# A hybrid encoder layer on one core: the first projection by input chunk, four output tiles side by side

## The chip, the cores and the metric

The kernel runs on one core of one Trainium2 chip. The metric is the time of one execution on the device in microseconds (us); lower is better. The numbers shown with a run are the median, the lowest and the highest of its executions. One more execution was recorded by the hardware profiler, instruction by instruction; its rows are what this document reads.

The engines are named as in the profile: PE (TensorE, matmuls), PEld (its weight loads), DVE (VectorE), ACT (ScalarE), POOL (GpSimd), SP (SyncE, which here only starts transfers). A queue with a small q behind the engine's name is the part of the engine that issues.

## What is computed

A layer takes x of 512 tokens by 1024 features (float32). One RMS-normalised input feeds three token mixers: an attention with forget gates ("fox"), a gated delta net ("gdn") and a stick-breaking attention. Their outputs are gated, summed and projected; then come a cross attention into 256 memory tokens and a gated MLP with a causal convolution. The change touches the input of the first mixer stage. From the reference, cut to that:

```python
h = rmsnorm(x, norm_mix[l])      # x * rsqrt(mean(x^2) + eps) * gain
(fq, fk, fv, ff, gq, gk, gv, gb, ga, gz, sq, sk, sv, gates) = split_projection(h @ w_in[l])
qkv = jax.nn.silu(causal_dwconv(jnp.concatenate([gq, gk, gv], axis=-1), gdn_conv[l]))
cq, ck, cv = jnp.split(qkv, [GDN_KW, 2 * GDN_KW], axis=-1)
o = gated_delta_rule(l2norm(heads(cq, GDN_HEADS)), l2norm(heads(ck, GDN_HEADS)),
                     heads(cv, GDN_HEADS), g_log, beta)
```

gq, gk and gv are 512 features each, that is four output tiles of 128 features by 512 tokens.

## The kernel before, in words

**Data and precision.** Features lie on partitions, tokens along the free axis. x arrives in eight chunks x0 to x7 of 128 x 512 (256 KB each). All dense weights arrive as a stream of units of 128 x 1024 float32 (512 KB) in the order of use. A unit of the gdn projections holds one output tile: its eight blocks of 128 x 128 belong to the eight input chunks, so one output tile needs one unit and all of x.

**Products.** A float32 value is kept as an exact sum of two fp32r values, high and low. For a unit, `split_unit` (L148) makes the high part with a copy on ACT (L154, whi) and the low part with a subtraction on DVE (L155, wlo). For an x chunk, `split_scaled` does it with the norm's gain multiplied in (xh on ACT L167, xl on DVE L168). `mm3` (L171) adds three products per chunk: high by high (L175), high weights by low x (L176), low weights by high x (L178). So `project` (L183) issues 24 matmuls of 128 x 512 for an output tile.

**Buffers.** PSUM has three pools: three "dense" buffers for projections, three "misc" ones and two of the gdn stage. The weight stream has three raw buffers, two of high parts and two of low parts.

**The start.** SP issues every transfer: x0, then the packed parameters cols (L281), the first gk unit in two halves (L142, L143), and so on with x and the next units between each other, and last the constants const (L285). ACT's first instruction is the load of a function table (L111). For each x chunk the kernel makes xh, xl and the square (L296), and DVE sums the squares (L298). A matmul with ones gives their sum over features (xps, L301); a logarithm, an exponential, a square on ACT and a Newton step on DVE make r_x, the norm's factor for each token (L303).

**Projections.** `project_conv` does gk, gq and gv by `ORDER`, a string of steps: K (gk), k (its convolution), Q, q, N (normalise), V, v, R (per-head scalars) and so on. gk and gq are "deferred": they use x times gain, and r_x is multiplied in when PSUM is evicted (L337, DVE). gv and all later projections use the normalised input, which `normalize` makes in one go for the eight chunks: scale by gain and r_x on DVE (L322), high part on ACT (L323), low part on DVE (L324). gv is evicted by a plain copy on ACT (L339). The convolution of a tile is one product on ACT (L347) and three multiply-adds on DVE (L349); its silu runs in place on ACT, four tiles behind one table load (`in_one_go`, L117).

**Who sets the order.** A tile scheduler orders the instructions of each engine by dependence, priority and a simulated timeline. Where the program says so (`keep_in_program_order`, `issue_after`), it keeps the written order. So a change in one place can move instructions at others.

Of the kernel before, what the change touches and what calls it, by code (L numbers as in the profile page):

```python
# [21 lines left out]
DEFERRED = ("gk", "gq")  # L22
CROSS = "k0 q0 k1 q1 w0 k2 q2 w1 k3 q3 w2 w3 v"
ORDER = """K k Q q N V v R F0 p0 p1 f0 S0 p2 p3 F1 s0 e f1 F2 f2 A0 C0 l0 F3 l1 l2 S1 l3 S2 f3 s1 n0
# [7 lines left out]
H = 4  # L32
# [34 lines left out]
def build(nc, tc, ctx, x_t, mem_t, w, cols_d, const_d, unit_d, out_t, dbg=None):  # L67
# [14 lines left out]
    work = tiles_of("work", "n", 4)        # short-lived  # L82
# [22 lines left out]

    def dump(name, ap):
        if dbg is not None and name in dbg:
            nc.sync.dma_start(dbg[name], ap)
# [28 lines left out]
    units = {}  # L137

    def load_unit(u):
        raw = wp.tile([P, 1024], F32, tag="wraw", name=f"wraw{u}", bufs=WB[0])  # L140
        if u == 0:
            nc.sync.dma_start(raw[:, :T], w[u, :, :T])  # L142
            nc.sync.dma_start(raw[:, T:], w[u, :, T:])  # L143
        else:
            nc.sync.dma_start(raw, w[u])
        return raw

    def split_unit(u):  # L148
        """a unit of the weight stream as an exact sum of two float32r operands"""
        raw = units.pop(u) if u in units else load_unit(u)  # L150
        hi = wp.tile([P, 1024], F32R, tag="whi", name=f"whi{u}", bufs=WB[1])
        lo = wp.tile([P, 1024], F32R, tag="wlo", name=f"wlo{u}", bufs=WB[2])
        for s in [slice(0, T), slice(T, 2 * T)] if u == 0 else [slice(0, 2 * T)]:
            S.activation(hi[:, s], raw[:, s], AF.Copy)  # L154
            V.tensor_tensor(lo[:, s], raw[:, s], hi[:, s].bitcast(F32), ALU.subtract)  # L155
        return hi, lo

    def split(src, alloc, name):
        """src as hi + lo"""
# [11 lines left out]
    def mm3(ps, unit, blocks, xs, first, last):  # L171
        """ps += the blocks of a unit times xs, without the product of the low parts"""
# [30 lines left out]
    def project_heads(u, ys, name, n=4):  # L203
        """[512, 1024] weights, two output tiles in a unit"""
# [7 lines left out]
    def rsqrt(ps, name, scale, n=T, work=work):  # L212
        """-2 / sqrt(ps * scale + eps), with a Newton step"""
# [9 lines left out]
    def head_norm(src, name, scale, n=T, work=work, psum=misc_ps, light=False):  # L223
        """-2 / sqrt(sum of src^2 * scale + eps) on every partition"""
# [62 lines left out]
    V.tensor_scalar(gains, gains, -0.5, None, ALU.mult)  # L287
    G.memset(ones, 1.0)
    V.tensor_copy(ones_r, ones)

# [1 line left out]
    xs, acc = [], None  # L292
    for k in range(KC):
        sq = work(f"xsq{k}")
        xs.append(split_scaled(hs[k], gkeep(f"xh{k}", F32R), gkeep(f"xl{k}", F32R), col("norm_mix", k)))
        S.activation(sq, hs[k], AF.Square)  # L296
        if acc is not None:
            V.tensor_tensor(sq, sq, acc, ALU.add)  # L298
        acc = sq
    ps = misc_ps("xps")  # L300
    PE.matmul(ps, ones, acc, start=True, stop=True)  # L301
    r_x = cp.tile([P, T], F32, tag="rh", name="r_x")
    V.tensor_scalar(r_x, rsqrt(ps, "rx", 1.0 / D), -0.5, None, ALU.mult)  # L303
# [4 lines left out]
    V.tensor_copy(ident_b, ident)  # L308
    mkt = cp.tile([P, P], BF16, tag="mkt", name="mkt")
    V.tensor_copy(mkt, cst("mask_t"))  # L310
    mkt2 = mkt[:, None, :].to_broadcast([P, 4, P])

    def v4(t):
        return t.rearrange("p (a b) -> p a b", a=4)

    def normalize():
        for k in range(KC):
            if k % 4 == 0:
                two = hquad(f"hh{k // 4}", F32R), hquad(f"hl{k // 4}", F32R)
            hi, lo = two[0][:, k % 4], two[1][:, k % 4]  # L320
            t = hs[k]
            V.scalar_tensor_tensor(t, t, col("norm_mix", k), r_x, ALU.mult, ALU.mult)  # L322
            S.activation(hi, t, AF.Copy)  # L323
            V.tensor_tensor(lo, t, hi.bitcast(F32), ALU.subtract)  # L324
            hs[k] = hi, lo
# [5 lines left out]
    def project_conv(g):  # L331
        raws[g] = []
        for h in range(H):
            u = UNITS[g] + h
            t = ytile(f"{g}u{h}")
            if g in DEFERRED:
                V.tensor_tensor(t, project(u, xs, f"{g}{h}"), r_x, ALU.mult)  # L337
            else:
                S.activation(t, project(u, hs, f"{g}{h}"), AF.Copy)  # L339
            raws[g].append(t)  # L340

    def convolve(g, base):
        """silu(conv(projection)) of the tiles of q, k or v"""
# [17 lines left out]
    def scalars():  # L361
# [16 lines left out]
        S.activation(ncoef[:R], col("row_alog", 0, 0, R), AF.Exp)  # L378
# [8 lines left out]
        # token on partition: [.., token block, row]  # L387
# [5 lines left out]
        # beta, beta * exp(gc), exp(g_last - gc)  # L393
# [4 lines left out]
    def select(ps, kind, h, stop=True):  # L398
        """a row of the scalars on every partition"""
# [5 lines left out]
        if kind == "-c":  # L405
            V.tensor_scalar(sel[:R], unit(h), -1.0, None, ALU.mult)
        else:
            V.tensor_copy(sel[:R], unit(64 + h))
# [11 lines left out]
    def prep_head(h):  # L420
# [6 lines left out]
        # the decay, [j, i] by chunks, 0 for j > i  # L427
# [13 lines left out]
        # A^T without its factors beta_i, and attn^T  # L441
# [15 lines left out]
        # token-major keys and values  # L457
# [13 lines left out]
    # the inverses of the 32 x 32 diagonal blocks of I + A by elimination, a block's  # L471
    # even or odd columns on a partition
# [30 lines left out]
    def expand(dst, src, h):  # L503
        """the 32 x 32 blocks of a head on the diagonals of its chunks"""
# [63 lines left out]
    def qkv_head(u, h, name, norm, alloc):  # L568
        """q^T, k^T and [key, dv] by key blocks"""
# [20 lines left out]
    def packed(name, kinds):  # L590
        """[P, 128], .. [P, 512] of each kind, the halves of a kind's tile shared"""
# [78 lines left out]
    tri_r = cp.tile([P, 2, P], F32R, tag="tri_r", name="tri_r")  # L670
    V.tensor_copy(tri_r[:, 0], cst("tri"))
# [61 lines left out]
    for step in ORDER.split():  # L733
# [5 lines left out]
         "N": lambda h: normalize(), "R": lambda h: scalars(), "z": lambda h: silu_gate(),  # L739
# [187 lines left out]
def unit_columns():  # L927
    """[P, 32, 16]: the even (on even partitions) or odd columns of the unit matrix"""
# [4 lines left out]
def layout(inputs):  # L933
# [3 lines left out]
    def tiles(a, n):  # L937
        """[K, M] -> [units, P, 1024] streaming (output tile, k chunk) blocks of [P, 128]"""
# [88 lines left out]
```

## Time and profile before

| | us |
|---|---|
| median of three runs | 1073.2 |
| lowest, highest | 1072.76, 1074.09 |
| span of the profiled execution | 1072.4 |
| PE busy | 1055.4 (98%) |
| DVE busy | 638.3 (60%) |
| ACT busy | 556.3 (52%) |

The profiled execution is not timed apart from its profile; its span from the first to the last instruction is 1072.4 us, 0.8 us under the median of the runs. A share of busy time is an average over the whole span. A row of a timeline gives the start and the duration of one instruction or of a few like ones in a row, then engine, line, operation, the tile written and the tiles read, and in brackets how long the engine stood before it and for whom. Matmuls are pipelined and their ends are modelled, so the distance between two starts says more than a duration.

### The profile page before, as it was taken

What the parts mean: (1) busy time and instruction counts of PE and PEld (TensorE: products, weight loads), DVE (VectorE), ACT (ScalarE), POOL (GpSimd) and SP (SyncE); (2) the same over time, 40 slices, a digit from 0 to 9 for tenths busy, and PEclk for the clock granted to TensorE, in tenths of its full rate; (3) what the DMA queues carried; (4) which work ended last, traced back from release to release, by engine and by line L of the source; (5) the groups of instructions that cost most, each with busy time, mean ns of one, the idle gap of its engine ahead of it and who ended that gap; (6) DMA issues with size and microseconds to landing.
All of it is one profiled execution on the core that took longest, in us unless ns stands there. A gap on an engine that the chain in (4) does not pass through costs nothing.

```text
span 1072.4 us, 12705 instructions
## 1 busy us (share of the span) xinstructions
PE 1055.4 (98%) x4868; PEld 858.3 (80%) x4868; DVE 638.3 (60%) x1002; ACT 556.3 (52%) x894; POOL 31.6 (3%) x81
## 2 busy tenths in 40 slices
PE   6999999999999999999999998999999999999998
PEld 4887888778888888888888886778888888888886
DVE  5987566886454443454577667667776667742221
ACT  6689677856263646574546557544444444431110
POOL 0000100101010000000000000000000000000000
PEclk9999999999999999999999999999999999999999
DMA  5232212121211122122244233122222222233330
GB/s 209 79 98 98 79 61 77 61 88 59 80 59 60 59 64 74 60 65 97 94 147 168 90 107 99 41 97 99 90 90 95 98 99 92 91 103 108 118 117 20
DMA packets 27853, 96.33 MB, mean 90 GB/s; under 512 B 3088, under 2 KB 3344, under 8 KB 27536
## 3 DMA queue, kind: packets, MB, share of 16 engines
q1 hardware_dynamic: 27648, 95.26, 27.1%
q8 instruction: 38, 0.62, 0.2%
q10 hardware_dynamic: 144, 0.26, 0.1%
q14 instruction: 23, 0.19, 0.1%
HBM read 93.41 MB, written 2.10 MB: 89 GB/s over the span
## 4 chain that ended last, share of the span: by engine, by line
PE 96%; DVE 1%; ACT 1%; DMA 1%; issue 0%; SPq 0%; DVEq 0%; ACTq 0%
PE up L176 8%; PE up L178 8%; PE up L175 8%; PE g L176 4%; PE g L175 4%; PE g L178 4%; PE dn L178 4%; PE dn L176 4%; PE dn L175 4%; PE wo L176 1%; PE s L175 1%; PE f L178 1%; PE f L175 1%; PE s L176 1%; PE wo L178 1%; PE wo L175 1%
## 5 line engine op out<-in xcount | busy, mean ns | idle before, releaser
L154 ACT ACTIVATE whi<-wraw 128x1024 fp32r<-128x1024 f32 (+1 forms) x168 | 177.1, 1054 | 286.0 <-PE up L176 86.1
L155 DVE TENSOR_TENSOR wlo<-wraw,whi 128x1024 fp32r<-128x1024 f32 (+1 forms) x168 | 204.7, 1219 | 144.2 <-PE dn L178 49.2
L176 PE MATMUL up<-xfl,whi 128*128 128x512 f32 x352 | 139.3, 396 | 0.0
L175 PE MATMUL up<-xfh,whi 128*128 128x512 f32 x352 | 138.7, 394 | 0.0
L178 PE MATMUL up<-xfh,wlo 128*128 128x512 f32 x352 | 88.9, 395 | 0.0
L178 PEld LDWEIGHTS up<-xfh,wlo 128*128 128x128 f32 x352 | 66.3, 188 | 15.7 <-issue 0.2
L176 PEld LDWEIGHTS up<-xfl,whi 128*128 128x128 f32 x352 | 66.3, 188 | 15.7 <-issue 0.2
L175 PEld LDWEIGHTS up<-xfh,whi 128*128 128x128 f32 x352 | 66.3, 188 | 15.5
L175 PE MATMUL g<-hh,whi 128*128 128x512 f32 x192 | 76.9, 401 | 0.0
L176 PE MATMUL g<-hl,whi 128*128 128x512 f32 x192 | 76.8, 400 | 0.0
L889 DVE SCALAR_TENSOR_TENSOR uc<-u,cols,uc 128x511 f32<-128x511 f32 (+1 forms) x88 | 65.3, 747 | 1.4
L887 ACT ACTIVATE uc<-u,cols 128x512 f32<-128x512 f32 x44 | 35.8, 816 | 45.2 <-DVE u L885 45.0
L885 DVE TENSOR_TENSOR u<-up,r_f 128x512 f32<-128x512 f32 x44 | 30.2, 688 | 40.4 <-PE up L178 40.4
L178 PE MATMUL g<-hh,wlo 128*128 128x512 f32 x192 | 52.3, 402 | 0.0
L178 PEld LDWEIGHTS g<-hh,wlo 128*128 128x128 f32 x192 | 35.9, 188 | 8.3 <-issue 0.2
L176 PEld LDWEIGHTS g<-hl,whi 128*128 128x128 f32 x192 | 36.2, 188 | 7.8 <-issue 0.2
L175 PEld LDWEIGHTS g<-hh,whi 128*128 128x128 f32 x192 | 36.2, 188 | 7.7
L175 PE MATMUL f<-hh,whi 128*128 128x512 f32 x64 | 26.0, 406 | 0.0
L175 PE MATMUL s<-hh,whi 128*128 128x512 f32 x64 | 25.7, 402 | 0.0
L176 PE MATMUL s<-hl,whi 128*128 128x512 f32 x64 | 25.5, 398 | 0.0
L176 PE MATMUL wo<-msl,whi 128*128 128x512 f32 x64 | 25.3, 396 | 0.0
L176 PE MATMUL f<-hl,whi 128*128 128x512 f32 x64 | 25.3, 395 | 0.0
(968 smaller groups left out, 2288.1 us busy)
## 6 DMA issues: line engine op xcount, KB each, us to landing
wraw<-w SPq DMA_DIRECT2D x166, 512.0 KB, 3.3
x<-x_t SPq DMA_DIRECT2D x8, 256.0 KB, 7.2
xr<-x_t SPq DMA_DIRECT2D x2, 1024.0 KB, 6.2
out<-out SPq DMA_DIRECT2D x8, 256.0 KB, 2.0
mem_sb<-mem_t SPq DMA_DIRECT2D x4, 256.0 KB, 6.5
wraw<-w SPq DMA_DIRECT2D x2, 256.0 KB, 4.7
inv<-unit ACTq DMA_DIRECT2D x1, 256.0 KB, 3.9
const<-const SPq DMA_DIRECT2D x1, 194.0 KB, 6.4
```

What stands on the lines that cost most here:

```text
L154: S.activation(hi[:, s], raw[:, s], AF.Copy)
L155: V.tensor_tensor(lo[:, s], raw[:, s], hi[:, s].bitcast(F32), ALU.subtract)
L175: PE.matmul(ps, hi[:, b], xh, start=first and i == 0, stop=False)
L176: PE.matmul(ps, hi[:, b], xl, start=False, stop=False)
L178: PE.matmul(ps, lo[:, b], xh, start=False, stop=last and i == len(xs) - 1)
L885: V.tensor_tensor(u, ps, r_f, ALU.mult)
L887: S.activation(c, u, AF.Identity, bias=col("ffn_conv_b", j), scale=col("ffn_conv", 3 * j + 2))
L889: V.scalar_tensor_tensor(c[:, s:], u[:, :T - s], col("ffn_conv", 3 * j + 2 - s), c[:, s:], ALU.mult, ALU.add)
```

## The change

- A small transfer `gains0` (128 x 8, the norm's gains) goes first on SP. Then come the eight x chunks, and only then cols and const.
- The gk weights are laid out by input chunk (`tokens`): a unit now holds two input chunks, each with 512 output features. Each unit comes in two halves of 128 x 512. The halves of the first three units are issued by ACT, those of the fourth by SP.
- Nine matmuls of constants (`WARM`, ones_r by ones_r into the buffer of xps) stand ahead of the first gk product.
- The four gk tiles are accumulated side by side in two dense and two gdn buffers. For each chunk: high part of the weights and xh on ACT, low part and xl on DVE, then twelve matmuls; the squares follow one chunk behind. All of this is pinned in the written order. xps follows behind the last gk product.
- Small DVE operations on constants, which the scheduler had put between the sums of squares, are pinned behind r_x.
- gq and gv both use x times gain, and both are evicted by DVE with r_x multiplied in.
- `normalize` works on one chunk. A table puts the chunks behind the evictions of gq1, gq2, gq3, gv0 and gv1; the step N is gone from `ORDER`.

The diff, without comments and with what the prediction speaks of:

```diff
-DEFERRED = ("gk", "gq")
+WARM = 9
+NORMALIZE = {"gq1": (0, 1), "gq2": (2,), "gq3": (3, 4), "gv0": (5,), "gv1": (6, 7)}
-ORDER = """K k Q q N V v R F0 ...
+ORDER = """K k Q q V v R F0 ...
...
+    gains0 = cp.tile([P, KC], F32, tag="gains0", name="gains0")
+    nc.sync.dma_start(gains0, cols_d[:, COLS["norm_mix"]:COLS["norm_mix"] + KC])
     hs = []
     for k in range(KC):
         t = ptile(f"x{k}")
         nc.sync.dma_start(t, x_t[:, k])
         hs.append(t)
-        if k == 0:
-            nc.sync.dma_start(cols, cols_d)
-        if k in (0, 2, 5):
-            u = UNITS["gk"] + len(units)
-            units[u] = load_unit(u)
-    nc.sync.dma_start(const, const_d)
+    def load_chunks(g, queue):
+        raw = wp.tile([P, 1024], F32, tag="wraw", name=f"wraw{g}", bufs=WB[0])
+        for q in range(2):
+            queue.dma_start(raw[:, q * T:q * T + T], w[UNITS["gk"] + g, :, q * T:q * T + T])
+        return raw
+    chunk_raws = [load_chunks(g, nc.scalar) for g in range(3)]
     exp_ln_tables()
...
+    nc.sync.dma_start(cols, cols_d)
+    nc.sync.dma_start(const, const_d)
+    ps_x = misc_ps("xps")
+    for _ in range(WARM):
+        PE.matmul(v4(ps_x), ones_r, ones_r[:, None, :].to_broadcast([P, 4, P]), start=True, stop=True)
+    first = [dense_ps("gk0"), dense_ps("gk1"), gdn_ps("gk2"), gdn_ps("gk3")]
...
+        pin(S.activation(hi[:, s], raw[:, s], AF.Copy))
+        pin(S.activation(xh, hs[k], AF.Copy, scale=gain))
+        pin(V.tensor_tensor(lo[:, s], raw[:, s], hi[:, s].bitcast(F32), ALU.subtract))
+        pin(V.scalar_tensor_tensor(xl, hs[k], gain, xh.bitcast(F32), ALU.mult, ALU.subtract))
+        if k:
+            add_squares(k - 1)
+        for a, b in ((hi, xh), (lo, xh), (hi, xl)):
+            for h in range(H):
+                c = q * T + h * P
+                pin(PE.matmul(first[h], a[:, c:c + P], b, start=k == 0 and a is hi and b is xh, stop=k == KC - 1 and b is xl))
+    add_squares(KC - 1)
+    pin(PE.matmul(ps_x, ones, sums[-1], start=True, stop=True))
...
-            if g in DEFERRED:
-                V.tensor_tensor(t, project(u, xs, f"{g}{h}"), r_x, ALU.mult)
+            if g == "gk":
+                V.tensor_tensor(t, first[h], r_x, ALU.mult)
             else:
-                S.activation(t, project(u, hs, f"{g}{h}"), AF.Copy)
+                evict = V.tensor_tensor(t, project(u, xs, f"{g}{h}"), r_x, ALU.mult)
+                with tc.issue_after(evict.ins):
+                    for k in NORMALIZE.get(f"{g}{h}", ()):
+                        normalize(k)
...
-    put("gk", tiles(wi[:, 2052:2564], 4))
+    put("gk", tokens(wi[:, 2052:2564]))
```

How the change moves instructions shows at three places.

The first is the start of ACT's queue, before and then changed. In brackets are the semaphores that an instruction waits for; DMAHW ones are counted up by transfers that have landed, eight of them in turn (DMAHW1 by gains0, DMAHW3 by the second half of the first unit). wraw is a raw unit, ghi its high part.

```order
L111 ACT_TABLE_LOAD
L296 ACTIVATE xsq_121<-x_92 128x512 [waits DMAHW0_49]
L167 ACTIVATE xh_122<-x_92,cols 128x512 [waits DMAHW1_49]
L378 ACTIVATE ncoef<-cols 96x1
L154 ACTIVATE whi_204<-wraw_95 128x512 [waits DMAHW2_49]
L154 ACTIVATE whi_204<-wraw_95 128x512 [waits DMAHW3_49]
```

```order
L283 DMA wraw_110<-w 128x512 x2
L283 DMA wraw_113<-w 128x512 x2
L283 DMA wraw_116<-w 128x512 [waits DMAHW1_49]
L283 DMA wraw_116<-w 128x512 [waits DMAHW3_49]
L115 ACT_TABLE_LOAD
L318 ACTIVATE ghi_138<-wraw_110 128x512 [waits DMAHW0_49]
L319 ACTIVATE xh_140<-x_94,gains_92 128x512 [waits DMAHW2_49]
```

The table load, first before, now stands behind six issues, of which the last two wait.

The second place is DVE around r_x, before and then changed. gku is the evicted gk tile, identb, mkt, tri_r and sel_g are small constants.

```order
L219 SCALAR_TENSOR_TENSOR rxb<-xps,rxb 128x512
L220 SCALAR_TENSOR_TENSOR rxa<-rxb,rxa 128x512
L303 TENSOR_SCALAR r_x<-rxa 128x512
L337 TENSOR_TENSOR gku_202<-gk_203,r_x 128x512
L337 TENSOR_TENSOR gku_235<-gk_236,r_x 128x512
```

```order
L217 SCALAR_TENSOR_TENSOR rxa<-rxb,rxa 128x512
L331 TENSOR_SCALAR r_x<-rxa 128x512
L332 TENSOR_SCALAR cols<-cols 128x5
L337 CAST identb<-const 128x128
L339 CAST mkt<-const 128x128
L702 CAST tri_r<-const 128x128
L439 CAST sel_g_954<-const 96x128
L439 CAST sel_g_1042<-const 96x128
L364 TENSOR_TENSOR gku_342<-gk_134,r_x 128x512
```

Six small operations have come between r_x and the first eviction.

The third place is ACT where the norms of the gdn heads (gkn0, gqn0) meet the silus of gk, gq and gv, before and then changed.

```order
L117 ACTIVATE gk_333<-gk_333 128x512
L111 ACT_TABLE_LOAD
L347 ACTIVATE gq_489<-gqu_421,cols 128x512
L154 ACTIVATE whi_610<-wraw_608 128x1024
L216 ACTIVATE gkn0a<-gkn0p,cols 128x512
L217 ACTIVATE gkn0a<-gkn0a 128x512
L218 ACTIVATE gkn0b<-gkn0a 128x512
L347 ACTIVATE gq_490<-gqu_454,cols 128x512
L117 ACT_TABLE_LOAD
```

```order
L350 ACTIVATE hh_521<-x_104 128x512
L213 ACT_TABLE_LOAD
L213 ACTIVATE gkn0a<-gkn0p,cols 128x512
L151 ACTIVATE whi_720<-wraw_718 128x1024
L214 ACT_TABLE_LOAD
L214 ACTIVATE gkn0a<-gkn0a 128x512
L215 ACTIVATE gkn0b<-gkn0a 128x512
L223 ACTIVATE gqn0s<-gq_526 128x512
L121 ACT_TABLE_LOAD
L121 ACTIVATE gq_528<-gq_528 128x512
```

The logarithm and the exponential of gkn0 now each have a load of their own. Up to the last silu of the gv tiles ACT's queue held 9 table loads before and holds 13 now.

## Rows read from the trace of the kernel before

**Rows 1.** The page: busy time of each engine; then the chain that ended last.

```profile
PE 1055.4 (98%) x4868; PEld 858.3 (80%) x4868; DVE 638.3 (60%) x1002; ACT 556.3 (52%) x894; POOL 31.6 (3%) x81
...
PE 96%; DVE 1%; ACT 1%; DMA 1%; issue 0%; SPq 0%; DVEq 0%; ACTq 0%
```

**Rows 2.** Waits of PE: us in total, times, longest us.

```profile
PE gk L175 <- ACT whi L154: 6.4, 2, 6.2
...
PE mT L840 <- DVE mp L836: 2.5, 1, 2.5
```

**Rows 3.** Waits of PE between 30 and 640 us.

```profile
PE pk L446 <- DVE gqn3b L219: 0.3, 1, 0.3
```

**Rows 4.** Timeline of SP's issues at the start: start us, duration us, what.

```profile
0.81 0.39 SPq L278 DMA_DIRECT2D x<-x_t  x1
```

**Rows 5.** Timeline of ACT at the start.

```profile
3.89 0.63 ACT L296 ACTIVATE xsq<-x 128x512 f32<-128x512 f32 x1 [1.80 <-DMA x<-x_t]
...
7.90 0.63 ACT L154 ACTIVATE whi<-wraw 128x512 fp32r<-128x512 f32 x1 [1.78 <-DMA wraw<-w]
9.19 0.72 ACT L167 ACTIVATE xh<-x,cols 128x512 fp32r<-128x512 f32 x1 [0.66 <-DMA x<-x_t]
```

**Rows 6.** Timeline of PE, start to the first matmul of gq.

```profile
9.96 0.79 PE L175 MATMUL gk<-xh,whi 128*128 128x512 f32 x1 [2.57 <-ACT xh L167]
...
13.23 0.63 PE L176 MATMUL gk<-xl,whi 128*128 128x512 f32 x1
13.66 0.63 PE L175 MATMUL gk<-xh,whi 128*128 128x512 f32 x1
...
24.64 1.02 PE L301 MATMUL xps<-xsq,ones 128*128 128x512 f32 x2
...
34.82 2.03 PE L178 MATMUL gk<-xh,wlo 128*128 128x512 f32 x8
36.69 0.40 PE L175 MATMUL gq<-xh,whi 128*128 128x512 f32 x1
```

**Rows 7.** Windows: busy us (instructions) of each engine, granted clock, DMA engines' share, GB/s.

```profile
0.00:4.00 4.00, 0.00 (x0) 0.00 (x0) 0.36 (x2) 1.39 (x2) 0.42 (x5) 1.00 0.48 140
4.00:8.00 4.00, 1.22 (x2) 0.50 (x2) 1.61 (x3) 1.96 (x5) 0.00 (x0) 1.00 0.76 209
```

**Rows 8.** Timeline of DVE at the start.

```profile
1.05 0.23 DVE L289 CAST ones_r<-ones 128x128 fp32r<-128x128 f32 x1 [1.05 <-POOL ones L288]
```

**Rows 9.** Timeline of PE in the cross attention, on both sides of its wait for mp.

```profile
662.73 1.89 PE L829 MATMUL msc<-memk,mqT 128*128 128x256 f32 x8
...
668.01 3.50 PE L829 MATMUL msc<-memk,mqT 128*128 128x256 f32 x8 [0.30 <-DVE mm L834]
```

**Rows 10.** Windows, the stretch of the second of these groups; columns as in rows 7.

```profile
668.00:671.00 3.00, 2.99 (x7) 2.47 (x8) 1.45 (x4) 0.34 (x1) 0.00 (x0) 0.50 0.00 0
```

**Rows 11.** Groups of DVE's instructions, 12 to 24 us: busy us, mean ns, idle before.

```profile
L168 DVE SCALAR_TENSOR_TENSOR xl<-x,cols,xh 128x512 fp32r<-128x512 f32 x6 | 4.5, 744 | 0.0
...
L671 DVE CAST tri_r<-const 128x128 fp32r<-128x128 f32 x1 | 0.2, 218 | 0.0
```

**Rows 12.** Timeline around r_x: ACT's first step and DVE's first evictions behind it.

```profile
25.69 0.69 ACT L216 ACTIVATE rxa<-xps,cols 128x512 f32<-128x512 f32 x1 [1.61 <-PE xps L301]
...
29.66 1.29 DVE L337 TENSOR_TENSOR gku<-gk,r_x 128x512 f32<-128x512 f32 x2
```

**Rows 13.** Groups of ACT's instructions, 60 to 100 us, columns as in rows 11.

```profile
L154 ACT ACTIVATE whi<-wraw 128x1024 fp32r<-128x1024 f32 x7 | 7.4, 1052 | 1.4 <-PE gv L176 1.4
L117 ACT ACT_TABLE_LOAD x3 | 3.8, 1283 | 0.1
...
L339 ACT ACTIVATE gvu<-gv 128x512 f32<-128x512 f32 x4 | 2.4, 596 | 2.3 <-PE gv L178 2.3
```

**Rows 14.** Windows of 10 us from 60 to 120: the fourth, and the sum of the six.

```profile
90.00:100.00 10.00, 10.00 (x47) 8.15 (x46) 4.93 (x7) 9.81 (x13) 0.00 (x0) 1.00 0.15 52
...
sum 60.00, PE 60.00 PEld 47.98 DVE 42.61 ACT 50.26 POOL 2.89; mean PE 10.00 PEld 8.00 DVE 7.10 ACT 8.38 POOL 0.48
```

More of the change, by code (lines that the diff above doesn't have):

```diff
@@ L104, in gdn_ps, with v4 @@
         return pg.tile([P, T], F32, tag="g", name=name)
+    def v4(t):
+        return t.rearrange("p (a b) -> p a b", a=4)
     def dump(name, ap):
@@ L134, in build @@
     ones_r = cp.tile([P, P], F32R, tag="ones_r", name="ones_r")
-    units = {}
     def load_unit(u):
         raw = wp.tile([P, 1024], F32, tag="wraw", name=f"wraw{u}", bufs=WB[0])
[L141 to L145, printed above, removed]
+        nc.sync.dma_start(raw, w[u])
         return raw
     def split_unit(u):
-        raw = units.pop(u) if u in units else load_unit(u)
+        raw = load_unit(u)
         hi = wp.tile([P, 1024], F32R, tag="whi", name=f"whi{u}", bufs=WB[1])
         lo = wp.tile([P, 1024], F32R, tag="wlo", name=f"wlo{u}", bufs=WB[2])
-        for s in [slice(0, T), slice(T, 2 * T)] if u == 0 else [slice(0, 2 * T)]:
-            S.activation(hi[:, s], raw[:, s], AF.Copy)
-            V.tensor_tensor(lo[:, s], raw[:, s], hi[:, s].bitcast(F32), ALU.subtract)
+        S.activation(hi, raw, AF.Copy)
+        V.tensor_tensor(lo, raw, hi.bitcast(F32), ALU.subtract)
         return hi, lo
@@ L286, in build @@
     exp_ln_tables()
-    V.tensor_scalar(gains, gains, -0.5, None, ALU.mult)
     G.memset(ones, 1.0)
     V.tensor_copy(ones_r, ones)
-    xs, acc = [], None
-    for k in range(KC):
[L294 to L301, printed above, removed]
+    nc.sync.dma_start(cols, cols_d)
@@ new lines, in build, with add_squares @@
+    nc.sync.dma_start(const, const_d)
[3 more added lines that the diff above has]
+    first = [dense_ps("gk0"), dense_ps("gk1"), gdn_ps("gk2"), gdn_ps("gk3")]
+    pin = tc.keep_in_program_order
+    xs, sums = [], []
+    def add_squares(k):
+        sq = work(f"xsq{k}")
+        pin(S.activation(sq, hs[k], AF.Square))
+        if sums:
+            pin(V.tensor_tensor(sq, sq, sums[-1], ALU.add))
+        sums.append(sq)
@@ new lines, in build @@
+    for k in range(KC):
+        g, q = divmod(k, 2)
+        if q == 0:
+            raw = chunk_raws[g] if g < 3 else load_chunks(g, nc.sync)
+            hi = wp.tile([P, 1024], F32R, tag="whi", name=f"ghi{g}", bufs=WB[1])
+            lo = wp.tile([P, 1024], F32R, tag="wlo", name=f"glo{g}", bufs=WB[2])
+        s = slice(q * T, q * T + T)
+        xh, xl = gkeep(f"xh{k}", F32R), gkeep(f"xl{k}", F32R)
+        xs.append((xh, xl))
+        gain = gains0[:, k:k + 1]
+        pin(S.activation(hi[:, s], raw[:, s], AF.Copy))
[8 more added lines that the diff above has]
+                pin(PE.matmul(first[h], a[:, c:c + P], b, start=k == 0 and a is hi and b is xh, stop=k == KC - 1 and b is xl))
@@ L302, in build @@
+    add_squares(KC - 1)
+    pin(PE.matmul(ps_x, ones, sums[-1], start=True, stop=True))
     r_x = cp.tile([P, T], F32, tag="rh", name="r_x")
-    V.tensor_scalar(r_x, rsqrt(ps, "rx", 1.0 / D), -0.5, None, ALU.mult)
+    V.tensor_scalar(r_x, rsqrt(ps_x, "rx", 1.0 / D), -0.5, None, ALU.mult)
+    pin(V.tensor_scalar(gains, gains, -0.5, None, ALU.mult))
     gl = cp.tile([P, H, 4], F32, tag="gl", name="gl")
@@ L307, in build, with normalize @@
     ident_b = cp.tile([P, P], BF16, tag="identb", name="identb")
-    V.tensor_copy(ident_b, ident)
+    pin(V.tensor_copy(ident_b, ident))
     mkt = cp.tile([P, P], BF16, tag="mkt", name="mkt")
-    V.tensor_copy(mkt, cst("mask_t"))
+    consts_in = pin(V.tensor_copy(mkt, cst("mask_t")))
     mkt2 = mkt[:, None, :].to_broadcast([P, 4, P])
[L313 to L325, printed above, removed]
+    halves = []
+    def normalize(k):
+        if k % 4 == 0:
+            halves[:] = hquad(f"hh{k // 4}", F32R), hquad(f"hl{k // 4}", F32R)
+        hi, lo = halves[0][:, k % 4], halves[1][:, k % 4]
+        t = hs[k]
+        V.scalar_tensor_tensor(t, t, gains0[:, k:k + 1], r_x, ALU.mult, ALU.mult)
+        S.activation(hi, t, AF.Copy)
+        V.tensor_tensor(lo, t, hi.bitcast(F32), ALU.subtract)
+        hs[k] = hi, lo
     conv = {}
@@ L403, in unit @@
             return ident[:R, r:r + 1].to_broadcast([R, P])
[L405 to L408, printed above, removed]
+        with tc.issue_after(consts_in.ins):
+            if kind == "-c":
+                V.tensor_scalar(sel[:R], unit(h), -1.0, None, ALU.mult)
+            else:
+                V.tensor_copy(sel[:R], unit(64 + h))
         PE.matmul(ps, sel[:R], rh[:R], start=True, stop=False)
```

8 lines of the change are left out of this document (4 added, 4 removed).

## The prediction, made before the changed kernel had run

> **What bounds the kernel now.** I read the page's head and its chain first: PE is busy for 98% of a span of 1072.4 us, and the chain of waits lies on PE for 96% of it [rows 1]. So an edit is worth what it does to PE's idle time, to PE's clock or to the number of PE's passes, and nothing else. The projection matmuls are as many as before.
>
> Next I read PE's waits. Over the whole run those of any size are at the start, all in gk (6.4 us on the copies of the weights and more on xh), and ahead of mT with 2.5 us [rows 2]. Between 30 and 640 us one wait of 0.3 us is left [rows 3]. This reads in two ways: the start is the place where something can be won, and behind it lies a long stretch in which nothing can be won and any delay would be new.
>
> At the start the timelines show what PE waits for. x0 is issued at 0.81 [rows 4] and used at 3.89; the second half of the first gk unit is used at 7.90, x1 at 9.19 [rows 5], and PE, after two matmuls, stands until 9.96 [rows 6]. Its early matmuls follow each other at 0.43 us (13.23 to 13.66), later ones at 0.234 us (eight between 34.82 and 36.69): the 1.2 and the 2.4 GHz level. gq0 begins at 36.69. Four gk tiles are 4 x 24 = 96 matmuls, at 0.234 us 22.4 us, and the sum of squares xps takes 1.0 us [rows 6]. So 36.7 - 22.4 - 1.0 = 13.3 us ahead of gq0 are lost to waiting and to the slow clock. The start can give no more than this.
>
> **The change, part by part. When gk begins.** PE's first gk matmul needs the first half unit and x0 in their fp32r copies from ACT. But ACT stands behind its own DMA issues: the order shows that its sixth waits for the landing of the second half of the first unit (call this moment L), and that the table load stands behind it. After L come an issue (0.4, as SP's [rows 4]), the table load (1.28 [rows 13]), a half copy (0.63) and xh (0.72 [rows 5]): L + 3.0 us.
>
> L is not in the trace of before. Low end: ACT's second issue goes out at about 1.3 us, two issues behind its start, and x0, the first transfer of before, was used 3.0 us after its issue: L = 4.3. High end: the same half stood fourth on one queue in before and was used at 7.90, so 7.9. Between them I count bytes. With this landing x0, x1 and two halves have come on two queues, 4 x 256 KB = 1.05 MB. The core moved 140 GB/s from 0 to 4 us (0.56 MB) and 209 GB/s from 4 to 8 [rows 7], so the other 0.49 MB take 2.3 us more: L = 6.3. I take this value, since it uses the rates of the very stretch. gk begins at 9.3.
>
> **Constant products.** ones_r is written at 1.05 + 0.23 us [rows 8], so nine products at 0.43 us run from 1.3 to 5.2, in time in which PE was idle. What they could buy is the clock. In before, PE stood for 2.5 us ahead of mT [rows 2]; the granted clock was then 0.50 [rows 10], and eight msc matmuls took 3.50 us where the eight of the head before had taken 1.89 [rows 9]. Here PE stands for 9.3 - 5.2 = 4.1 us, longer than that, so I book those 1.6 us once for gk. If the gap is shorter than 2.5 us, nothing is booked.
>
> **gk itself.** A chunk gives PE 12 matmuls, 2.8 us at the fast level. ACT has a half copy, xh and a square for it (0.63 + 0.72 + 0.63 = 2.0 [rows 5]), DVE a subtraction, xl and an addition, 2.2 us if each takes as long as xl (0.744 [rows 11]). Both stay below PE. A chunk's data, 0.52 MB in 2.8 us, is 187 GB/s, below the 209 of 4 to 8 us. So after its start gk runs without waits, and gq0 can begin at 9.3 + 22.4 + 1.6 + 1.0 = 34.3 instead of 36.7. **Term 1: -2.4 us** (bounds -6.0 and -0.8, worked out in the rivals).
>
> **gq1's buffer.** There are three dense buffers. gk0, gk1 and gq0 fill them, so gq1 waits for gk0's eviction, which needs r_x. In before the chain from the first logarithm to that eviction took 29.66 - 25.69 = 4.0 us [rows 12] and lay beside gk1 to gk3. Now xps stands at the end of gk. After it come these 4.0 us, the six small DVE operations that are now pinned between r_x and the eviction (at 0.22 each [rows 11], 1.3) and the eviction (0.65, half of the pair at 29.66 [rows 12]): 5.95 us; a unit's copy in front of the logarithm adds between 0 and 1.05 [rows 13]. gq0 covers 24 x 0.234 = 5.6. The new wait is 0.35 to 1.4 us. **Term 2: +0.9 us**, the middle.
>
> **What follows r_x.** DVE's work behind r_x (evictions, convolution, normalisation) starts at 34.3 + 4.0 + 0.5 + 1.3 = 40.1 instead of 29.66: 10.4 us later, while PE is 2 us earlier. In before, from 60 to 120 us, DVE is free for 60 - 42.6 = 17.4 us and ACT for 60 - 50.3 = 9.7 [rows 14]. The change gives DVE four gv evictions more, 4 x 0.65 = 2.6 us, which leave ACT (4 x 0.60 = 2.4 [rows 13]). Normalising chunk by chunk adds no instruction. But the order shows 13 table loads on ACT up to the gv tiles' last silu, where before had 9; at 1.28 us each [rows 13] these are 5.1 us more, net +2.7 on ACT.
>
> Is this late work covered? DVE has 17.4 - 2.6 = 14.8 us against 10.4 of lateness: covered by 120 us. ACT has 9.7 - 2.7 = 7.0: some 3.4 us of lateness remain, and ACT's queue also holds the copies of the units that PE consumes, with two buffers between. Low end 0: the two buffers (two units, 11.2 us of PE) take it all. High end: the added work of both engines, 2.7 + 2.6 = 5.3 us, shows on PE in full. As one engine is covered and the other not, I take the middle. **Term 3: +2.65 us.** That gq and gv read raw x takes a dependence away from PE, which waited for nothing there; it has no term of its own. The rest of the kernel is the same.
>
> Sum: -2.4 + 0.9 + 2.65 = +1.15. The profiled execution's span is 1072.4 us; the median of the three runs is 1073.2, with 0.8 us around that span. So 1073.2 + 1.15 = **1074.4 us**, within 0.2% of before (1071.1 to 1075.3), which is about what a measurement of this kernel can tell from no change.
>
> **The rivals. Early start, faster.** L = 4.3, so gk begins at 7.3; PE stands only 2.1 us behind the constant products, less than the 2.5 us that lost the clock. gq0 begins at 7.3 + 22.4 + 1.0 = 30.7, a gain of 6.0. With term 2, and term 3 between 0 and 2.65, the net is -5.1 to -2.45: 1068.1 to 1070.8, say 1069.4. For it: x0 was used 3.0 us after its issue although the columns and the first unit were issued right behind it. Against it: x1, the fifth in that queue, was used only at 9.19 [rows 5].
>
> **Late evictions, slower.** The start is as forecast, but ACT's queue, at 9.81 of 10 us from 90 to 100 [rows 14], can't take four more table loads; unit copies and evictions behind them hold PE, and term 3 is 5.3. Net -2.4 + 0.9 + 5.3 = +3.8: 1077.0. It decides once ACT is late by more than the two units of cover, 11.2 us, at any place behind 80 us. For it: ACT's missing 3.4 us. Against it: that cover, and no wait of PE in before though ACT was full there.
>
> **The second queue brings nothing, slower too.** The transfers share what the core can move and L is as late as in before, 7.9. gk begins at 10.9 and gq0 at 10.9 + 22.4 + 1.6 + 1.0 = 35.9, a gain of 0.8. Net -0.8 + 0.9 + 2.65 = +2.75: 1076.0. For it: only 140 and 209 GB/s in the first 8 us. Against it: the DMA engines' share was only 0.48 and 0.76 there [rows 7], so they had room. The Trainium skill (DMA: Bandwidth & Descriptors, Issuing engines are not separate DMA queues) speaks against the change and for this rival: transfers started by different engines run on the same 16 DMA engines, and starting them on several saves only the time of issuing. No run here shows yet which it is.
>
> **How the numbers follow.** Forecast 0.36 (its own range is 1072 to 1077), early start 0.32, late evictions 0.20, no use of the second queue 0.12. Faster by over 0.2%: nearly all of the early start, 0.31. Same: two thirds of the forecast and a little from the others, 0.32. Slower: the rest, 0.37. The range, 1068.5 to 1078.5, leaves out an early start for which nothing is paid later, and both slow cases at once.
>
> **What would show it.** Right: PE's first gk matmul at 9 to 10 us and some matmuls at 0.43 us behind it, gq0 near 34.3, a wait of about 1 us ahead of gq1 that DVE's gku ends, and a few waits of together 2 to 3 us between 80 and 320 us. Wrong in term 1: gk at 7 to 8 us and at 0.234 from the first matmul. Wrong in term 3: no waits there, or waits of 5 us and more, with table loads on ACT ahead of the instruction that ends them.

## The result, and the profile after the change

The changed kernel takes 1078.15 us (median of 4 runs, 1077.17 to 1078.26), the kernel before 1073.38 on the same chip: ratio 1.0042, 95% interval 1.0028 to 1.0056. It is slower, by 4.8 us between the medians. In every run the time is 1.7 us above its span, so the profiled execution of before (span 1072.4) is its slowest of four; that of after has a span of 1076.4.

First the chain on the page of after. The answer to [rows 1]: PE is still busy for 98% of the span, and its share of the chain has gone from 96% to 94%. The page alone doesn't explain a change of this size.

```profile
PE 94%; ACT 3%; DVE 1%; DMA 0%; issue 0%; ACTq 0%
```

PE's waits of after, whole run (us in total, times, longest), the answer to [rows 2, 3].

```profile
PE gk L327 <- ACT xh L319: 3.0, 1, 3.0
PE mT L871 <- DVE mp L867: 2.5, 1, 2.5
PE g L172 <- ACT gate L687: 1.6, 1, 1.6
...
PE fn13p L230 <- DVE fn13l L160: 1.2, 1, 1.2
PE sz L714 <- ACT f L618: 0.8, 1, 0.8
...
PE pu L546 <- DVE y L561: 0.8, 1, 0.8
PE f L172 <- ACT svt L613: 0.5, 1, 0.5
PE fT L661 <- DVE fd L657: 0.3, 1, 0.3
```

Two things stand here. The start's wait has shrunk. And six new waits, g, fn13p, sz, pu, f and fT, have appeared between 125 and 317 us, together 5.2 us, where before had 0.3.

The start on PE and ACT (timelines), the answer to [rows 5, 6]:

```profile
1.33 4.21 PE L296 MATMUL xps<-ones_r 128*128 128x512 f32 x9 [1.33 <-DVE ones_r L289]
8.49 2.08 PE L327 MATMUL gk<-xh,ghi 128*128 128x512 f32 x4 [2.95 <-ACT xh L319]
...
13.62 1.08 PE L327 MATMUL gk<-xh,ghi 128*128 128x512 f32 x4
...
33.60 0.79 PE L172 MATMUL gq<-xh,whi 128*128 128x512 f32 x1
```

```profile
0.81 5.06 ACTq L283 DMA_DIRECT2D wraw<-w  x6
5.90 1.28 ACT L115 ACT_TABLE_LOAD   x1 [5.90 <-DMA wraw<-w]
7.20 0.63 ACT L318 ACTIVATE ghi<-wraw 128x512 fp32r<-128x512 f32 x1
7.73 0.70 ACT L319 ACTIVATE xh<-x,gains 128x512 fp32r<-128x512 f32 x1
```

ACT's last issue ends at 5.87, behind the landing; the table load, the half copy and xh follow, and gk begins at 8.49. The first twelve gk matmuls (three groups of four) take 13.62 - 8.49 = 5.1 us, the lower clock, where twelve at 0.234 take 2.8. gq0 begins at 33.60, 3.1 us earlier than in [rows 6]. So the start won 3.1 us, and 3.1 + 4.0 (the difference of the two spans) = 7.1 us went later: 4.9 of them are the new waits less the 0.3 of before, and 2.2 are not in rows of waits. Part of these is the way a wait is counted, from the modelled end of the matmul ahead of it. From start to start, the six matmuls behind the waits come 6.3 us later than the 0.23 us (512 columns) or 0.11 us (128) at which such matmuls otherwise follow each other, and the one of before comes 0.5 us later. So 5.8 of the 7.1 us lie at the waits and some 1.3 elsewhere. All of it is lost by 515 us, in the stretch where the two orders differ: on2p, which comes behind it, begins on PE at 511.04 in before and at 514.87 in after, 3.8 us apart, and the matmuls behind it keep that distance to the end. The granted clock is no cause, since no 4 us of after between 36 and 600 us have less than 1.00. The rest of 1.3 us stays open.

### The profile page after: what moved, and what is told of

It reads as the page before. It is cut to its first block, busy times and chain, and to the rows that moved or that the text cites. A ratio compares the mean times of both kernels' runs of the same rounds, so it can differ in the third digit from the quotient of the medians.

```text
span 1076.4 us, 12738 instructions
## 1 busy us (share of the span) xinstructions
PE 1059.3 (98%) x4877; PEld 861.7 (80%) x4877; DVE 642.4 (60%) x1009; ACT 557.2 (52%) x897; POOL 33.9 (3%) x81
## 4 chain that ended last, share of the span: by engine, by line
PE 94%; ACT 3%; DVE 1%; DMA 0%; issue 0%; ACTq 0%
PE up L175 8%; PE up L172 8%; PE up L173 8%; PE g L172 4%; PE g L173 4%; PE g L175 4%; PE dn L175 4%; PE dn L172 4%; PE dn L173 4%; PE gk L327 2%; PE f L172 1%; PE wo L173 1%; PE wo L175 1%; PE s L173 1%; PE f L175 1%; PE s L172 1%
## 5 line engine op out<-in xcount | busy, mean ns | idle before, releaser
L151 ACT ACTIVATE whi<-wraw 128x1024 fp32r<-128x1024 f32 x163 | 172.5, 1058 | 276.8 <-PE up L173 86.1
L152 DVE TENSOR_TENSOR wlo<-wraw,whi 128x1024 fp32r<-128x1024 f32 x163 | 199.4, 1223 | 132.5 <-PE dn L175 49.2
```

Of the source, the lines that this page charges most:

```text
L151: S.activation(hi, raw, AF.Copy)
L152: V.tensor_tensor(lo, raw, hi.bitcast(F32), ALU.subtract)
```

## The experiments

Each is the changed kernel with the edit named, unless it says otherwise. All were timed against the kernel before (medians 1073.15 to 1073.55 us).

### The start: warm17 and table_first

```diff
-WARM = 9
+WARM = 17
```

> The changed kernel with 17 constant products instead of 9, so that they run until 1.3 + 17 x 0.43 = 8.6 us, when gk begins (8.49). Theory A (PE's 2.95 us of standing behind the constant products costs the clock, and what is won at the start reaches the end): the first twelve gk matmuls, which took 5.1 us, take 2.8, gq0 begins near 31.4 instead of 33.6, and the time falls by about 2.2 us to 1076. Rival B (the later waits are set by DVE and ACT, which stay where they are): gq0 begins earlier, the waits behind 120 us grow by as much, and the time stays at 1078.

Measured: 1077.02 us, ratio 1.0033 (1.0021 to 1.0046).

```diff
+    exp_ln_tables()
     chunk_raws = [load_chunks(g, nc.scalar) for g in range(3)]
-    exp_ln_tables()
```

> The changed kernel with ACT's table load ahead of its six issues. If the table load behind the landing of the first unit costs its 1.28 us: gk begins at about 7.2 to 7.7 instead of 8.49, PE stands less than 2.2 us behind the constant products, which by my reading of the clock keeps it; gq0 near 30.3 and the time near 1075. If instead the later issues delay the landing by as much as the load took: gk stays near 8.5 and the time at 1078.

Measured: 1076.13 us, ratio 1.0019 (1.0010 to 1.0028). The starts of gk on PE, first warm17, then table_first:

```profile
1.33 5.59 PE L296 MATMUL xps<-ones_r 128*128 128x512 f32 x17 [1.33 <-DVE ones_r L289]
8.90 1.20 PE L327 MATMUL gk<-xh,ghi 128*128 128x512 f32 x4 [1.98 <-ACT xh L319]
```

```profile
7.24 1.39 PE L327 MATMUL gk<-xh,ghi 128*128 128x512 f32 x4 [2.05 <-ACT xh L319]
8.43 1.91 PE L327 MATMUL gk<-xh,glo 128*128 128x512 f32 x4
```

Seventeen products take 5.59 us where nine took 4.21, so the last of them already follow each other at the faster level. warm17 has it from the first gk matmul; gq0 begins at 31.78, 1.8 us earlier than in after. table_first has gk at 7.24 but loses the clock after four matmuls; gq0 at 31.66, 1.9 us earlier. The late waits of both are those of after to 0.1 us; of table_first:

```profile
PE g L172 <- ACT gate L687: 1.6, 1, 1.6
```

So the late waits don't depend on when the start is done. What table_first won at the start reaches the end (2.0 us between the medians). Of warm17's 1.8 us the medians show 1.1. Its profiled execution is the slowest of its five (1078.73): on2p begins there at 513.23, still 1.6 us earlier than in after, and the gain is lost behind 675 us, which I didn't resolve.

### start_tuned: both

> The changed kernel with ACT's table load ahead of its issues and with 17 constant products. The products end near 6.9 us and gk begins near 7.3, so the clock holds: the first twelve gk matmuls take 2.8 us instead of 4.9 in table_first, unless the second x chunk, which came at 9.0 there, holds them up. gq0 near 31, the later waits of 5.2 us unchanged, time 1074 to 1075. If the waits grow by what the start gains: 1076.

Measured: 1075.23 us, ratio 1.0013 (1.0004 to 1.0022); gq0 at 30.81, 2.8 us earlier than in after, the time 2.9 us shorter, and the late waits once more the same. With 5.9 us won at the start over before, the kernel is still slower than it.

### Halves of the change: start_only and rest_only

start_only puts N back into the order of steps and evicts gv, made from the normalised input, on ACT. rest_only is the kernel before with:

```diff
-DEFERRED = ("gk", "gq")
+DEFERRED = ("gk", "gq", "gv")
+NORMALIZE = {"gq1": (0, 1), "gq2": (2,), "gq3": (3, 4), "gv0": (5,), "gv1": (6, 7)}
-ORDER = """K k Q q N V v ...
+ORDER = """K k Q q V v ...
```

and normalize by chunk behind the evictions.

> The changed kernel with its start, but gv from the normalised input with its eviction on ACT and the normalisation in one go, as before. Theory C (the waits behind 120 us, together 5.2 us, come from the order that values on raw x and the normalisation in pieces have led to): they go, the start's 3.1 us are kept, about 1071. Rival D (they come from r_x's work starting some 8 us later): DVE has to normalise all chunks ahead of gv with less time, a wait of 1 to 4 us appears ahead of gv, and the time is 1075 to 1080.

> The kernel before with its start, and of the change only that gv uses x times gain with eviction on DVE and that the chunks are normalised behind the evictions. Theory C (the order and the added work make the waits): waits of 3 to 6 us between 80 and 320 us, time 1076 to 1079. Rival D (the lateness makes them): PE waits there as little as in before, 1073 to 1074.

Measured: 1085.18 us, ratio 1.0108 (1.0094 to 1.0122), and 1087.03 us, ratio 1.0124 (1.0107 to 1.0140). Both are worse than the whole change, beyond anything expected. Three waits of start_only:

```profile
PE sc L587 <- ACT m L567: 2.5, 1, 2.5
PE gqn3p L229 <- ACT gqn3h L159: 1.8, 1, 1.8
PE g L172 <- ACT whi L151: 1.8, 1, 1.8
```

rest_only has the same three (sc, gqn3p and g, 2.5, 1.8 and 1.8 us), in a kernel whose start is 3.3 us later (gq0 at 36.19 and 32.85) and whose gv is made in another way. Behind the waits the clock falls too: start_only has it at 0.50 from 200 to 206 and from 377.5 to 380.5 us, rest_only at 0.56 and 0.52 from 200 to 207 and from 378 to 385, where after has 1.00. What the two kernels share is a third order of the later part: from some point on the scheduler had given both the same one. So neither half can be priced as long as the scheduler may choose anew with each edit. That led to the next experiments, which hold the order.

### Holding the order: old_order and rest_old_order

The instructions traced from the fox queries of head 0 on are the same ones in all these kernels. A table holds their numbers in the order of the kernel before, for PE, ACT, DVE and POOL, and each is queued behind its predecessor. What is traced ahead of them (gq, gv, their convolutions and the scalars) the scheduler still orders as it likes:

```diff
+LATE = {"PE": """137-138 154-155 0-23 ...""", "ACT": ..., "DVE": ..., "POOL": ...}
...
+    for order in LATE.values():
+        last = None
+        for run in order.split():
+            a, _, b = run.partition("-")
+            for k in range(int(a), int(b or a) + 1):
+                if last is not None:
+                    tc.add_manual_dep(number[zero + k], last.name, behind, reason="order")
+                last = number[zero + k]
```

> The changed kernel, but behind the first product of the fox queries of head 0 the instructions of PE, ACT, DVE and POOL stand, engine by engine, in the order of the kernel before (a table of numbers that fixes it; what is computed stays). Theory O (the new order of the later part makes the waits): the waits behind 120 us go, the start's 3.1 us stay, 1070 to 1071. Theory L (the work behind r_x comes too late for PE, and the scheduler's new order only spreads that): the waits behind 120 us go too, but a wait of together 4 to 6 us appears where PE first needs that work, between 90 and 115 us, and the time is 1075 to 1077.

Measured: 1078.48 us, ratio 1.0048 (1.0035 to 1.0061): as slow as the change. PE's waits and ACT's timeline ahead of them:

```profile
PE fn00p L320 <- ACT fn00h L250: 3.3, 1, 3.3
...
PE rcol L511 <- DVE rows L502: 1.2, 1, 1.2
...
PE f L266 <- DVE wlo L243: 0.8, 1, 0.8
```

```profile
92.58 1.28 ACT L496 ACT_TABLE_LOAD   x1
...
94.53 1.28 ACT L497 ACT_TABLE_LOAD   x1
...
96.47 1.28 ACT L499 ACT_TABLE_LOAD   x1
97.77 0.20 ACT L499 ACTIVATE ncoef<-cols 96x1 f32<-96x1 f32 x1
97.99 1.28 ACT L212 ACT_TABLE_LOAD   x1
...
100.45 1.28 ACT L206 ACT_TABLE_LOAD   x1
101.74 0.63 ACT L314 ACTIVATE fn00s<-f 128x512 f32<-128x512 f32 x1
```

The waits of 125 to 317 us are gone, and 5.3 us of waits stand at 94 to 104 instead, where fn00 sits on ACT behind a row of five table loads. So the waits of after belong to its order, and this is theory L, with a time 1.5 us above its range. Here is where PE has rcol and fn00p in before:

```profile
98.37 0.50 PE L390 MATMUL rcol<-const,rows 96*128 96x96 f32 x4
...
101.05 0.40 PE L232 MATMUL fn00p<-fn00h,ones_r 128*128 128x512 f32 x1
```

In after they begin at 107.85 and 108.58. The scheduler had moved them to a place where PE doesn't wait for them, in an order whose waits come later.

> The run rest_only (start of before; gv from x times gain with eviction on DVE; chunks normalised behind the evictions) with the order of before fixed in the same way. Theory O: no waits behind 30 us beyond those of before, 1073 to 1074. Theory L, in the form that the four evictions more on DVE and the normalisation between the convolutions make the work behind r_x late by themselves: a wait of 5 to 9 us between 85 and 110 us, 1078 to 1082, against 1087 of rest_only.

Measured: 1082.62 us, ratio 1.0085 (1.0071 to 1.0098); one wait of this size:

```profile
PE gqn0p L324 <- ACT gqn0h L254: 7.4, 1, 7.4
```

So with the start of before, and its order from the fox queries on, the second half of the change (gv on raw x, normalising by pieces) makes PE wait for 7.4 us. That is inside theory L's range. It doesn't show that ACT and DVE had too much to do. gqn0p stands at 74.44 among the products of gv in before and at 94.28 behind all of them here, and ACT's part of it comes late in ACT's queue:

```profile
79.02 1.06 ACT L246 ACTIVATE whi<-wraw 128x1024 fp32r<-128x1024 f32 x1 [2.31 <-PE gv L268]
...
92.57 0.61 ACT L318 ACTIVATE gqn0s<-gq 128x512 f32<-128x512 f32 x1
```

gq, which gqn0s reads, was complete at 69.5, and ACT stood idle for 8 us in five pieces between 65 and 82. Four table loads came between 82.8 and 91.0, ahead of gqn0s. So an order that the scheduler chose, in the part that the table doesn't hold, stands behind this wait, and what the work alone would cost is not shown.

### What makes the late work late: ncoef_early, ncoef_old, rx_old

```diff
+    ncoef = cp.tile([P, 1], F32, tag="ncoef", name="ncoef")
+    pin(S.activation(ncoef[:96], col("row_alog", 0, 0, 96), AF.Exp))
     pin(PE.matmul(ps_x, ones, sums[-1], start=True, stop=True))
...
-        ncoef = cp.tile([P, 1], F32, tag="ncoef", name="ncoef")
-        pin(S.activation(ncoef[:R], col("row_alog", 0, 0, R), AF.Exp))
```

> The changed kernel with one thing moved: the exponential ncoef of the scalars stands at the end of gk, where ACT holds its table, instead of among the scalars, where it takes a table load of its own. The order of everything else is the same instruction by instruction. If ACT's additional loads make the waits behind 120 us (my prediction's slower rival): they shrink by up to 1.3 us, 1076.5 to 1077. If ACT has caught up by then and those waits are set by the order alone: the waits keep their sizes to 0.1 us and the time stays at 1078.

> old_order with the same move of ncoef. There PE's waits lie at 93 to 104 us (fn00p 3.3, rcol 1.2, f 0.8), right behind ACT's row of five table loads. If that row sets them: fn00p falls by about 1.3 us to 2, and the time by 1.5 to 2.5 (the slow clock behind the wait shrinks too) to 1076 to 1077. If DVE sets them: no change, 1078.5.

Measured: ncoef_early 1077.77 us, ratio 1.0045 (1.0032 to 1.0058), the late waits 1.6, 1.2, 0.9, 0.8, 0.5 and 0.3 as in after. ncoef_old 1076.26 us, ratio 1.0032 (1.0020 to 1.0044), with

```profile
PE fn00p L320 <- ACT fn00h L250: 2.0, 1, 2.0
...
PE rcol L511 <- DVE rows L502: 1.0, 1, 1.0
```

One table load fewer is worth nothing to the waits in the order of after and 1.3 us of fn00p's wait in the order of before. In after, ACT had caught up: it stands for 1.7 us for DVE at 116, ahead of the first of the six waits, and has no table load between 105 and 208 or between 241 and 371 us. In old_order the load was part of the wait. The six runs of ncoef_old spread from 1074.36 to 1078.97, and the profiled one is the fastest: the waits shown are those of that run, and the gain in time is only roughly known.

The load of ncoef is one that the change itself had made: in before ACT does ncoef at 5.04 us, under the first table, and the changed kernel pins it among the scalars.

rx_old is old_order with:

```diff
-        if k:
-            add_squares(k - 1)
+        add_squares(k)
...
-    add_squares(KC - 1)
-    pin(PE.matmul(ps_x, ones, sums[-1], start=True, stop=True))
```

and xps between the products of chunks 5 and 6.

> old_order with the sum of squares xps and with it r_x ahead of the last two chunks of gk, so that r_x is there some 5 us earlier. Theory L in the form of the prediction (the work behind r_x is late because r_x is late): the waits of 5.3 us at 93 to 104 us go almost wholly, 1072 to 1074. Theory W (between r_x and 100 us ACT and DVE have more work than PE's earlier start leaves them time for, whenever r_x comes): the waits move or change place but keep a sum of 4 to 6 us, 1077 to 1079.

Measured: 1076.77 us, ratio 1.0035 (1.0023 to 1.0047). r_x begins at 31.53 on DVE instead of 37.11 and is 5.6 us earlier; the waits are

```profile
PE f L266 <- DVE wlo L243: 2.4, 1, 2.4
PE gqn0p L321 <- DVE gqn0l L251: 1.7, 1, 1.7
PE fn00p L320 <- ACT fn00h L250: 1.5, 1, 1.5
```

together 5.6 us against 5.3. The sum stays, as theory W has it (the time is just below its range), so the lateness of r_x alone doesn't set these waits. That the amount of work on ACT and DVE sets them, the other half of W, is not shown. The order ahead of the fox queries came out differently again (gqn0p at 83.96, in old_order at 79.30), and DVE had time to spare ahead of the dearest wait, that for wlo:

```profile
95.91 0.69 DVE L507 SCALAR_TENSOR_TENSOR rows_u<-rows_u,rows_e 96x512 f32<-96x512 f32 x1 [2.90 <-ACT rows_e L506]
```

It stood for 2.9 us for a step of the scalars that ACT did behind two table loads (92.01 and 93.95), with wlo behind it in its queue. What both traces share is ACT from 90 to 100 us, busy for 9.88 of 10. The 1.7 us that rx_old is faster than old_order go with the clock: from 102 to 108 us old_order has it at 0.50 to 0.52, around fn00p's wait of 3.3 us, and rx_old keeps 1.00.

### Taking work away: relieved and relieved_2

```diff
-        V.tensor_tensor(lo, t, hi.bitcast(F32), ALU.subtract)
+        G.tensor_tensor(lo, t, hi.bitcast(F32), ALU.subtract)
         hs[k] = hi, lo
```

with the start of start_tuned, xps as in rx_old and the constants' operations in chunk 6.

> start_tuned with three edits that bring the work behind r_x forward and take it from DVE: the sum of squares xps and r_x stand ahead of the last two chunks of gk instead of behind gk, the constants' operations stand in chunk 6 instead of behind r_x, and the low parts of the normalised chunks (eight subtractions) are made by POOL. Theory L: the lateness falls by some 5 us for r_x and 6 us of DVE's work, PE's later waits fall to at most 2 us, and the time is 1067 to 1070, below before. Theory O: the waits change by chance with the order, 1071 to 1080.

Measured: 1073.58 us, ratio 1.0001 (0.9993 to 1.0010): as before, not faster, though gq0 begins at 30.71. Theory L's forecast missed, and the time lies in theory O's range. The waits of 125 to 317 us are gone, and these are left:

```profile
PE rcol L435 <- DVE rows L426: 2.2, 1, 2.2
...
PE fn00p L229 <- ACT fn00h L159: 0.9, 1, 0.9
...
PE gqn0p L229 <- ACT gqn0h L159: 0.5, 1, 0.5
```

Three edits were made at once, and the order was free: from 124 us on PE has the same sequence of operations and tiles as in before (compared instruction by instruction). So the six waits are gone here together with the order that they belong to, and which of the edits brought that about is not shown.

> relieved with ncoef early and the order of relieved fixed behind F0. In relieved PE waited 2.2 us for rows (DVE, behind ACT's loads for the scalars), 0.9 for fn00 and 0.5 for gqn0, and its clock was at 0.61 from 96 to 100 us. If those waits come from ACT's five loads at 88 to 98 us: rcol and fn00p fall below 1 us together, the clock stays, and the time is 1069 to 1071. If from DVE: 1073.

Measured: 1071.97 us (1070.38 to 1072.62, 11 runs), ratio 0.9986 (0.9978 to 0.9995). It is faster than before by 0.14%, and than the change by some 6 us. The windows of 96 to 100 us (columns as in [rows 7]), relieved and then relieved_2:

```profile
96.00:100.00 4.00, 3.61 (x13) 2.38 (x11) 1.53 (x2) 3.93 (x7) 0.00 (x0) 0.61 0.41 131
```

```profile
96.00:100.00 4.00, 2.66 (x12) 1.89 (x12) 1.77 (x3) 3.96 (x6) 0.00 (x0) 1.00 0.37 131
```

rcol's wait fell from 2.2 to 1.5, fn00p's grew from 0.9 to 1.3 and gqn0p's from 0.5 to 0.7: together 3.5 us against 3.6. The expectation of under 1 us for the first two missed, and the time is above its range: ACT is busy for 3.96 of 4 us there still. What is won is the clock, which stays at 1.00; why it stays is not shown.

## Why the prediction was right or wrong

The time lies in the range, 0.35 us inside its upper end, and not at the forecast of 1074.4. That it lies inside is partly luck: terms 1 and 2 came out 1.6 us better than booked, term 3 over 4 us worse. The slower rival "late evictions" (1077.0, chance 0.20) came nearest in time, but not by its mechanism: in after no table load lies within 20 us ahead of any of the six waits.

**When gk begins: right in kind, 0.8 us too late.** L + 3.0 held: ACT's last issue ended at 5.87, and as an issue takes 0.4, L was near 5.5; gk began at 8.49 instead of 9.3. L was earlier than my 6.3, between x0's 4.3 and that. The second queue was of use: 4 to 8 us shows

```profile
4.00:8.00 4.00, 1.54 (x4) 0.66 (x2) 0.14 (x1) 2.09 (x3) 0.00 (x0) 1.00 0.96 308
```

308 GB/s and a share of 0.96 against 209 and 0.76 [rows 7], in a kernel that also puts its transfers in another order. The rival "the second queue brings nothing" falls, since L was 5.5 and not 7.9. The Trainium skill's rule (DMA: Bandwidth & Descriptors, Issuing engines are not separate DMA queues) says that both queues share 16 engines, and that a second one saves only the time of issuing. The trace doesn't speak against it: here the engines had room, and the one queue of before was held up in issuing, with 2.98 us for three issues of otherwise 0.4:

```profile
4.09 2.98 SPq L278 DMA_DIRECT2D x<-x_t  x3
```

**Constant products: the step was wrong.** I booked 1.6 us for a clock that PE gets by the products and loses by standing. But the nine products, 4.21 us in all, follow each other at 0.43 us or more to the last, and so do the first twelve matmuls of gk: in this execution the faster level wasn't reached before 13.4 us, so there was nothing to lose. It cost 5.1 - 2.8 = 2.3 us. (The windows of after show a granted clock of 1.00 even there, and those of [rows 7] do too; ahead of the first change of level the starts of the matmuls tell it, not that column.) In old_order, with the same start, gk's first four matmuls take 1.72 us instead of 2.08 and the clock is 0.50 from 9.0 to 12.3: there the level had been reached, and was lost. **Term 1** was -3.1 against -2.4: gk began 0.8 us earlier, the lower clock cost 0.7 us more, and xps held PE for 0.5 us instead of 1.0.

**gq1's buffer: too dear.** From the first logarithm to the first eviction it took 4.6 us with the constants (34.30 to 38.87), where I had 5.3: the six small operations, each booked at 0.22, took 0.74 together (38.13 to 38.87), as they start 0.07 to 0.14 us apart. The logarithm began 0.1 us behind xps, as the unit's copy ahead of it ran beside xps, and no wait of PE for gku stands in the rows. Term 2 was near 0 instead of 0.9.

**What follows r_x: the step that failed.** It is term 3, "as one engine is covered and the other not, I take the middle", +2.65. It measured 7.1 us, of which 5.2 stand in rows of waits, above even my upper end of 5.3. Two things in it were wrong. I let the lateness fade as DVE and ACT found free time up to 120 us. But what counts is when PE needs a result, and in the order of before it needs gqn0, rcol and fn00 at 74 to 101 us, where DVE and ACT had little time free. From 70 to 90 us (columns as in [rows 7]) DVE has 9.77 and 9.29 of 10 us, and ACT has 9.35 in the second of these windows and 9.81 in the next [rows 14]:

```profile
70.00:80.00 10.00, 10.00 (x44) 8.10 (x43) 9.77 (x14) 7.58 (x11) 0.00 (x0) 1.00 0.32 105
80.00:90.00 10.00, 10.00 (x45) 7.45 (x43) 9.29 (x14) 9.35 (x14) 0.00 (x0) 1.00 0.31 107
```

With the later part in that order, old_order and rx_old show 5.3 and 5.6 us of waits between 84 and 104 us, with r_x at 37.1 and at 31.5. And I took the later order as given, though the scheduler makes it anew: it moved rcol by 9.5 us, and the six waits at 125 to 317 us belong to its new order, as old_order shows. At the dearest of them, the gate's, ACT had stood idle for PE 6 us earlier, so it wasn't behind with old work (timeline of after):

```profile
195.77 0.37 ACT L468 ACTIVATE et<-pt,ngc 128x128 f32<-128x128 f32 x1 [0.81 <-PE pt L464]
...
201.62 1.84 ACT L687 ACTIVATE gate<-g,cols 128x512 f32<-128x512 f32 x3
```

Of the table loads that the rival named, the one of ncoef costs time in the order of before (ncoef_old) and nothing in that of after (ncoef_early), and the next ones before the waits lie over 20 us ahead of them.

**The base.** I put 0.8 us around the span; it is 1.7 in each run, and the profiled execution of before took 1074.1 us.

What stays open: whether the waits between 84 and 104 us come from the amount of work on ACT and DVE or from the order that the scheduler gives it ahead of the fox queries, which no experiment held; how much of them each half of the change makes, since start_only and rest_only were given other orders; and the 1.3 us that lie at no wait.

## What to carry to other kernels

In this kernel, where PE is busy for 98%, a gain at the start was spent where the other engines' next results didn't come earlier by as much: ask for each first use on PE, not for free time on average. Where a scheduler orders the program, an edit at the start can change the order hundreds of microseconds later; hold that order, or compare it, before a difference is put down to the edit, and hold it from the edit on: a table that begins later leaves the part between free. A function table that is switched in the middle of a chain costs 1.28 us each time in ACT's queue, so small exponentials belong where the table is loaded already; whether PE feels it depends on the order (ncoef_old and ncoef_early).

## What the hardware showed that I had not expected

- PE's clock: behind nine constant products and 2.05 us of standing (table_first) it fell to the lower of its two levels after four matmuls; behind seventeen and 1.98 us (warm17) it stayed; and in after's execution nine products hadn't brought the upper level at all. A wait of 2.4 us at 98 us in rx_old left it at 1.00, one of 2.2 us in relieved was followed by 0.61. The length of a wait alone doesn't tell it.
- A subtraction of 128x512 took POOL 1.67 us on average in relieved, where DVE takes 0.69. And DVE was slower while POOL worked: the same subtraction for a unit's low part took 1.21 us without POOL, and 2.32 us beside two on POOL (62.15 to 65.20 us, and from 65.80 on):

```profile
59.15 1.21 DVE L152 TENSOR_TENSOR wlo<-wraw,whi 128x1024 fp32r<-128x1024 f32 x1
...
63.97 2.32 DVE L152 TENSOR_TENSOR wlo<-wraw,whi 128x1024 fp32r<-128x1024 f32 x1
```

Over the four stretches in which POOL worked, DVE's operations took some 7 us longer than their like elsewhere (an estimate from the distances of their starts), and the eight subtractions had cost DVE some 5 us. So that moving them paid is not shown.
